# One store of a batched matmul split by partitions, so that one of the 16 DMA engines moves nothing for it

## Chip, cores and metric

One core of one Trainium2 chip. The metric is the device time of one execution in microseconds (us), of the slowest core, which here is the only one. Before: 125.71 us, median of 3 runs (125.65 to 125.92). "Faster" and "slower" mean by over 2%.

## The reference

```python
batch, m, k, n = 16, 512, 512, 512          # a: [16, 512, 512], b: [16, 512, 512], float32
out = np.matmul(a, b.transpose(0, 2, 1))    # float32 [16, 512, 512]
```

33.55 MB are read and 16.78 MB written; one batch of the output is 1 MB, stored as 128 partitions of 8 KB.

## The kernel before

The five engines run hand-written streams that meet at semaphores: SP issues all loads and the stores 8 to 15, POOL issues the stores 0 to 7 through its software queue, DVE casts to bf16, TensorE transposes and multiplies, ACT evicts. The parts that the change and the argument touch:

```python
STORES = "SSSSOSOSOSSOOOOOO"                 # POOL: S = issue the next store, O = wait until one has landed
LATE = {11: (8, 9), 13: (10, 11), 15: (12, 13)}   # SP: stores issued once load 11, 13, 15 has landed

def load(n):                                 # 2 MB: two batches of a (n even) or of b (n odd)
    ...
    nc.sync.dma_start(ld[:, slot], src).then_inc(s_ld[slot], 16)

def landed(n):
    return s_st[n], 16

def store(n):
    engine = nc.gpsimd if n < STORES.count("S") else nc.sync
    engine.wait_ge(s_out, n + 1)
    engine.dma_start(
        out[n].rearrange("(p j) n -> p j n", j=J), ob[:, n % NO]     # 128 partitions x 8 KB
    ).then_inc(s_st[n], 16)
...
for n in range(2 * pairs):                   # SP
    ...                                      # wait for load n, issue load n + 6
    for m in LATE.get(n, ()):
        store(m)
store(batch - 2)
store(batch - 1)
```

Buffer `ob` has seven slots; the slot of store 12 is not written again.

## Time and profile before

| | before |
|---|---|
| time, median | 125.71 us |
| span in the profile | 124.2 us |
| compute done (last eviction ends) | 114.28 us |
| store 15: fifteenth / sixteenth semaphore increment | 120.98 / 122.74 us |
| one 8 KB row on one DMA engine | 0.309 us (one starts 0.306 after the other) |

In the trace each of the kernel's transfers raises its semaphore in 16 increments as its parts land (those of store 15 from 120.60 to 122.74 us); they are read here as one for each of the 16 DMA engines. The times of these increments, and the start and length of every DMA packet, are in the trace; they have no engine number. Times below count from the start of the span. The lines of the profile are in the prediction.

### The profile page before, as it was taken

To read this page: it belongs to the slowest core of one execution; us is meant where nothing else is said; L and a number is where in the kernel's file an instruction comes from. 1 tells how busy PE (TensorE), PEld (TensorE's weight loads), DVE (VectorE), ACT (ScalarE), POOL (GpSimd) and SP (SyncE) were. 2 spreads that over 40 slices of the span, in tenths; PEclk is the share of its full clock that TensorE was granted. 3 is DMA by queue.
4 is the path that set the end of the run, shared out by engine and by line. 5 is a ranking of instruction groups with operands and counts; after the bars stand their busy time and mean duration, and the time that the engine had idled before them with its cause. 6 is when DMAs were issued, how large, how long until landed. Compare 5 with 4: busy or idle time off the path is not lost. (4 is left out here: it accounts for less than half of the span.)

```text
span 124.2 us, 2416 instructions
## 1 busy us (share of the span) xinstructions
PE 92.5 (74%) x768; PEld 58.0 (47%) x768; DVE 70.0 (56%) x112; ACT 68.1 (55%) x130; POOL 6.2 (5%) x14
## 2 busy tenths in 40 slices
PE   0006299998999899899989998995699937995000
PEld 0005296467447644764575477343684426541000
DVE  0055676948992897589488578903968059400000
ACT  4005133679558946966695589435665196556000
POOL 2000000000000070002010220000000000000000
PEclk9999999999999999999999999999779999999965
DMA  4999999999999999999999999999999999999970
GB/s 84 401 425 430 443 438 428 433 428 422 428 428 428 428 438 420 401 430 430 414 425 433 430 438 417 435 435 412 454 414 433 409 430 425 430 430 425 428 327 8
DMA packets 4896, 50.33 MB, mean 405 GB/s; under 512 B 544, under 2 KB 544, under 8 KB 544
## 3 DMA queue, kind: packets, MB, share of 16 engines
q1 hardware_dynamic: 3744, 41.94, 80.2%
q0 software_dynamic: 1152, 8.39, 16.0%
HBM read 33.55 MB, written 16.78 MB: 405 GB/s over the span
## 5 line engine op out<-in xcount | busy, mean ns | idle before, releaser
L266 PE MATMUL ps<-tb,ta 128*128 128x512 bf16 x256 | 57.8, 379 | 0.4
L224 ACT COPY ob<-ps 128x512 f32 x64 | 34.4, 589 | 29.7 <-PE ps L266 26.6
L206 ACT COPY ta<-tp 128x512 bf16<-128x512 bf16 x64 | 32.9, 610 | 15.4 <-PE tp L247 15.4
L266 PEld LDWEIGHTS ps<-tb,ta 128*128 128x128 bf16 x256 | 24.2, 98 | 30.5 <-issue 3.9
L247 PE MATMUL tp<-ident,ha 128*128 128x128 bf16 x256 | 20.2, 236 | 12.6 <-PEq L148 12.6
L247 PE MATMUL tp<-ident,hb 128*128 128x128 bf16 x256 | 19.4, 236 | 8.1 <-PEq L148 7.9
L247 PEld LDWEIGHTS tp<-ident,ha 128*128 128x128 bf16 x256 | 17.5, 107 | 15.8 <-issue 14.1
L187 DVE COPY tb<-tp 128x1024 bf16<-128x1024 bf16 x32 | 21.3, 684 | 5.4 <-DVEq L148 5.3
L247 PEld LDWEIGHTS tp<-ident,hb 128*128 128x128 bf16 x256 | 17.2, 107 | 8.7 <-issue 8.7
L167 DVE CAST hb<-ld 128x1024 bf16 x8 | 5.5, 688 | 12.5 <-DVEq L148 12.3
L182 DVE COPY ha<-wa 128x2048 bf16<-128x2048 bf16 x8 | 5.5, 694 | 10.3 <-DVEq L148 10.1
L167 DVE CAST ha<-ld 128x1024 bf16 x8 | 5.5, 687 | 6.6 <-DVEq L148 6.5
L113 POOL DMA_DIRECT2D out_dram<-ob x8 | 5.5, 693 | 65.0 <-DMA ld<-in_b_dram 41.5
L172 DVE CAST hb<-ld 128x1024 bf16 x8 | 5.5, 685 | 1.1 <-DVEq L148 1.1
L172 DVE CAST ha<-ld 128x1024 bf16 x8 | 5.5, 688 | 1.0 <-DVEq L148 1.0
L186 DVE COPY hb<-wb 128x2048 bf16<-128x2048 bf16 x8 | 5.5, 685 | 0.5 <-DVEq L148 0.5
L170 DVE CAST wa<-ld 128x1024 bf16 x8 | 5.5, 686 | 0.0
L170 DVE CAST wb<-ld 128x1024 bf16 x8 | 5.5, 685 | 0.0
L175 DVE CAST wa<-ld 128x1024 bf16 x8 | 5.5, 684 | 0.0
L175 DVE CAST wb<-ld 128x1024 bf16 x8 | 5.5, 682 | 0.0
L197 ACT ACT_TABLE_LOAD x1 | 1.3, 1283 | 1.1 <-SPq L43 1.1
L80 POOL TENSOR_SCALAR_AFFINE_SELECT ident<-ident 128x128 bf16<-128x128 bf16 x1 | 0.3, 283 | 0.2 <-POOL ident L78 0.2
(6 smaller groups left out, 0.8 us busy)
## 6 DMA issues: line engine op xcount, KB each, us to landing
ld<-in_a_dram SPq DMA_DIRECT2D x7, 2048.0 KB, 29.9
ld<-in_b_dram SPq DMA_DIRECT2D x7, 2048.0 KB, 31.1
out_dram<-ob POOLq DMA_DIRECT2D x8, 1024.0 KB, 28.7
out_dram<-ob SPq DMA_DIRECT2D x8, 1024.0 KB, 20.4
ld<-in_a_dram SPq DMA_DIRECT2D x2, 1024.0 KB, 6.2
ld<-in_b_dram SPq DMA_DIRECT2D x2, 1024.0 KB, 10.2
```

What stands on the lines that cost most here:

```text
L113: engine.dma_start(out[n].rearrange("(p j) n -> p j n", j=J), ob[:, n % NO]).then_inc(s_st[n], 16)
L167: nc.vector.tensor_copy(out=h[:, :J, :], in_=src[:, :J, :HK]).then_inc(s_cd, 1)
L170: nc.vector.tensor_copy(out=w[:, :J, :], in_=src[:, :J, HK:])
L172: nc.vector.tensor_copy(out=h[:, J:, :], in_=src[:, J:, :HK]).then_inc(s_c, 1)
L175: nc.vector.tensor_copy(out=w[:, J:, :], in_=src[:, J:, HK:]).then_inc(s_w, 1)
L182: nc.vector.tensor_copy(out=ha[:], in_=wa[:]).then_inc(s_ca, 1)
L186: nc.vector.tensor_copy(out=hb[:], in_=wb[:]).then_inc(s_cb, 1)
L187: nc.vector.tensor_copy(out=tb[:, ko, :], in_=tp[:, 2 + ko % 2].rearrange("k j p -> k (j p)"),).then_inc(s_eb, 1)
L206: c = nc.scalar.copy(out=ta[:, ko, e * J * P:(e + 1) * J * P].rearrange("k (j p h) -> k j p h", j=J, h=2), in_=tp[:, ko % 2, :, e * HP:(e ...
L224: c = nc.scalar.copy(out=dst[:, j, :].rearrange("m (p j) -> m p j", j=2 * J), in_=ps[:, j, :].rearrange("m (j p) -> m p j", j=2 * J),)
L247: t = nc.tensor.transpose(tp[:, 2 * x + g, j, :], h[:, j, g * P:(g + 1) * P], ident[:])
L266: t = nc.tensor.matmul(ps[:, j, :], ta[:, ko, (e * J + j) * P:(e * J + j + 1) * P], tb[:, ko, :].rearrange("k (j p) -> k j p", j=2 * J)[:, ...
```

## The change: intent and diff

At the end of the kernel before one DMA engine runs 1.76 us behind the fifteen others. The change gives engine 15, taken for that one, nothing to do for one store: 120 partitions were expected to go to fifteen engines and the last eight to eight of these. As the trace has no engine numbers, those in this document are names: 0 to 7 are the eight that also get one of the last eight rows, 8 to 14 the other seven, 15 is the one left out.

```diff
+    FEWER = 12
...
         def landed(n):
-            return s_st[n], 16
+            return s_st[n], 32 if n == FEWER else 16
...
             engine.wait_ge(s_out, n + 1)
+            if n == FEWER:
+                dst, src = out[n].rearrange("(p j) n -> p j n", j=J), ob[:, n % NO]
+                for p, j in ((slice(0, 120), slice(0, J)), (slice(120, P), slice(0, J))):
+                    engine.dma_start(dst[p, j], src[p, j]).then_inc(s_st[n], 16)
+                return
```

## The prediction

> **What bounds the kernel now.** I read the page from the top, then the table of busy time by stretch (the stages, then the last 3 us in slices of 0.2 us), then the increments of each transfer's semaphore. First the page: busy shares, the row of DMA activity and the queues.
>
> ```profile
> span 124.2 us, 2416 instructions
> ...
> PE 92.5 (74%) x768; PEld 58.0 (47%) x768; DVE 70.0 (56%) x112; ACT 68.1 (55%) x130; POOL 6.2 (5%) x14
> ...
> DMA  4999999999999999999999999999999999999970
> GB/s 84 401 425 430 443 438 428 433 428 422 428 428 428 428 438 420 401 430 430 414 425 433 430 438 417 435 435 412 454 414 433 409 430 425 430 430 425 428 327 8
> ...
> q1 hardware_dynamic: 3744, 41.94, 80.2%
> q0 software_dynamic: 1152, 8.39, 16.0%
> ```
>
> No compute engine passes 74%. The 16 DMA engines are full from the second slice to the thirty-eighth, at some 428 GB/s: the kernel moves 50.33 MB and is bound by that. The two queues are the one of SP (all loads, and stores 8 to 15) and the software queue of POOL (stores 0 to 7).
>
> Next, when the compute work ends: the last eviction and the last store's issue, from the timeline.
>
> ```profile
> 113.70 0.58 ACT L224 COPY ob<-ps 128x512 f32 x1
> 114.31 0.33 SPq L113 DMA_DIRECT2D out_dram<-ob  x1
> ```
>
> After 114.64 us only transfers run. The span ends 9.5 us later, so the chain on the page, which stops at this eviction, doesn't show what the end waits for. The table by stretch does (the last two columns are the share of the 16 DMA engines and GB/s; a packet counts in the slice where it starts):
>
> ```profile
> 115.00:118.00 3.00, 0.00 (x0) 0.00 (x0) 0.00 (x0) 0.00 (x0) 0.00 (x0) 1.00 1.02 429
> ...
> 120.00:120.20 0.20, 0.00 (x0) 0.00 (x0) 0.00 (x0) 0.00 (x0) 0.00 (x0) 0.50 0.97 410
> 120.20:120.40 0.20, 0.00 (x0) 0.00 (x0) 0.00 (x0) 0.00 (x0) 0.00 (x0) 0.50 0.60 246
> 120.40:120.60 0.20, 0.00 (x0) 0.00 (x0) 0.00 (x0) 0.00 (x0) 0.00 (x0) 0.50 0.02 0
> 120.60:120.80 0.20, 0.00 (x0) 0.00 (x0) 0.00 (x0) 0.00 (x0) 0.00 (x0) 0.50 0.12 41
> 120.80:121.00 0.20, 0.00 (x0) 0.00 (x0) 0.00 (x0) 0.00 (x0) 0.00 (x0) 0.50 0.00 0
> 121.00:121.20 0.20, 0.00 (x0) 0.00 (x0) 0.00 (x0) 0.00 (x0) 0.00 (x0) 0.50 0.10 41
> 121.20:121.40 0.20, 0.00 (x0) 0.00 (x0) 0.00 (x0) 0.00 (x0) 0.00 (x0) 0.50 0.10 41
> 121.40:121.60 0.20, 0.00 (x0) 0.00 (x0) 0.00 (x0) 0.00 (x0) 0.00 (x0) 0.50 0.00 0
> 121.60:121.80 0.20, 0.00 (x0) 0.00 (x0) 0.00 (x0) 0.00 (x0) 0.00 (x0) 0.50 0.10 41
> 121.80:122.00 0.20, 0.00 (x0) 0.00 (x0) 0.00 (x0) 0.00 (x0) 0.00 (x0) 0.50 0.10 41
> ```
>
> 41 GB/s for 0.2 us is one packet of 8 KB. Up to 120.4 us all engines are at work; after it a single packet starts at a time, five in all, at 120.70, 121.04, 121.35, 121.65 and 121.96 us in the packet records, each of 0.31 to 0.34 us. That is one DMA engine with five rows left when the fifteen others are done: its packets end at 122.27 us, theirs at 120.66.
>
> The semaphore increments say the same, each transfer having 16 of them. Store 15: fifteen from 120.60 to 120.98 us, the sixteenth at 122.74. The instructions end at 124.17, 1.42 us after. Lag of the sixteenth behind the fifteenth, by transfer: 0.12 to 0.15 us in every load that lands before 48.2 us; then 0.40 in the load landing at 70.4, 0.72 at 85.3, 1.02 at 100.2; 1.51 in store 9, 1.71 in store 12, 1.76 in store 15. POOL issues its stores from 43.2 to 72 us and the last lands at 104.8. So the lag is built while the software queue works and is kept afterwards, when every store takes 2.45 us on all engines (eight rows of 0.306 each).
>
> [...] A row here goes at 8192 B / 0.306 us = 26.8 GB/s[...].
>
> **The change part by part.** Removed: the 8 rows of 8 KB that engine 15 moves for store 12, 8 x 0.309 = 2.47 us of its time. Added: one row more on each of engines 0 to 7, 0.31 us; one more issue on SP, 0.33 us by the row of the last store; one more semaphore packet on eight engines, 0.009 us each. Moved: nothing on the four compute engines (the order of their instructions is the same, and store 12's buffer is not written again).
>
> On the path that sets the end: the issue isn't, as stores 12 and 13 are issued some 10 us before their data moves, and store 15 at 114.31 with 3.6 us of rows in front of it (store 14's fifteen increments come by 118.54). The rows are. Engine 15, if it is the laggard, now ends its packets at 122.27 - 2.47 = 119.80. Engines 8 to 14 stay at 120.66 or before, engines 0 to 7 come to 120.66 + 0.31 = 120.97 at most. So the end moves from 122.27 to 120.7-121.0, a gain of 1.3 to 1.6 us. Taken from the landings: 122.74 to 120.98 + 0.31 = 121.29, 1.45 us. The 1.42 us behind the last landing stay. 125.71 - 1.45 = 124.26 us.
>
> **The rivals.**
> (A) *The last eight rows queue [...].* [...] four rows take 4 x 0.309 = 1.24 us in place of 0.31, and 1.55 [...]. Engines 0 to 7 then end at 121.9 to 122.2, and 0 to 0.4 us is left of the gain: 125.3 to 125.7. [...]
> (B) *The 120 partitions collide too.* [...] up to 8 x 0.309 = 2.47 us more for fifteen engines, some 2.1 after the 0.4 us by which the engines are offset. With (A): 120.66 + 2.1 + 1.2 = 124.0 against 122.27, so 1.7 us slower: 127.4. [...] Nothing in the profile speaks for or against.
> (C) *The laggard is another engine.* If it is 7 [...], it gets a row more: 126.0. If it is one of 8 to 14, nothing moves: 125.7. For it: the trace has no number. Against: the change is made to spare the highest engine, and in an already tuned kernel that is hardly by chance.
> (D) *Nothing shows, as the lag is hidden anyway.* Ruled out: nothing but the sixteenth increment holds SP at the end.
>
> **Range and chances.** Main path 124.3 (weight 0.5), A 125.4 (0.2), C 125.8 (0.05), B 127.4 (0.2) and its worst form 129 (0.05). The middle of these lies a little above the main path; I say 124.5, and 124.0 to 127.4 for eight in ten. Faster by over 2% would need under 123.2 us, more than the whole lag of 1.76 gives: 0.02. Slower by over 2% means over 128.2, which only the worst form of B reaches: 0.08. Within 2%: 0.90.
>
> **What would show each step.** Right: in the slices at the end no stretch with one packet at a time; the sixteenth increment of stores 13 to 15 within about 0.5 us of the fifteenth; of the two parts of store 12, the larger landing in about 2.45 us after store 11's; the last landing near 121.3 us. A would show as engines 0 to 7 up to 1.2 us behind engines 8 to 14 in store 13, B as a DMA rate well below 428 GB/s for 2 to 5 us around 111 to 116 us, and packets of over 0.309 us there; C as the same tail of single packets at the end. The prediction is wrong if the compute engines' times move at all, if the rate dips at store 12, or if the lag grows again after it.

## The result, and the profile after

128.70 us (median of 4 runs, 128.52 to 128.98) against 125.70: ratio 1.0237, 95% interval 1.0215 to 1.0260, so slower by over 2%. Ratios here and below are the mean time of one kernel's fast runs over that of the other's of the same rounds, so not quite the ratio of the medians quoted.

The page of the changed kernel, the lines that answer to those of before:

```profile
span 127.2 us, 2417 instructions
...
PE 92.6 (73%) x768; PEld 57.9 (46%) x768; DVE 70.0 (55%) x112; ACT 68.1 (54%) x130; POOL 6.2 (5%) x14
...
DMA  3999999999999999999999999999999999999910
GB/s 88 405 433 446 423 433 443 428 423 417 433 438 433 423 402 438 420 435 397 438 417 443 420 430 428 441 425 428 433 420 425 423 428 425 425 340 402 394 80 10
...
q1 hardware_dynamic: 3751, 41.94, 78.9%
q0 software_dynamic: 1152, 8.39, 15.6%
```

No compute engine's busy time moved by over 0.1 us, and the bytes are the same. SP's queue has 7 packets more (3751 against 3744): 23 semaphore packets (15 and 8) in place of 16, so the transfers do run on 15 and on 8 engines. New are the dip to 340 GB/s in slice 36 and a longer tail. By stretches of 1 us (last two columns: share of the DMA engines that is busy, GB/s):

```profile
110.00:111.00 1.00, 1.00 (x7) 0.42 (x5) 0.00 (x0) 0.84 (x2) 0.00 (x0) 1.00 1.03 434
111.00:112.00 1.00, 1.00 (x6) 0.46 (x5) 0.00 (x0) 0.47 (x1) 0.00 (x0) 1.00 1.02 410
112.00:113.00 1.00, 1.00 (x6) 0.48 (x5) 0.00 (x0) 0.60 (x2) 0.00 (x0) 1.00 1.02 360
113.00:114.00 1.00, 0.51 (x3) 0.01 (x1) 0.00 (x0) 0.80 (x2) 0.00 (x0) 1.00 1.07 303
114.00:115.00 1.00, 0.00 (x0) 0.00 (x0) 0.00 (x0) 0.29 (x1) 0.00 (x0) 1.00 0.92 352
...
121.00:122.00 1.00, 0.00 (x0) 0.00 (x0) 0.00 (x0) 0.00 (x0) 0.00 (x0) 0.50 0.33 139
122.00:123.00 1.00, 0.00 (x0) 0.00 (x0) 0.00 (x0) 0.00 (x0) 0.00 (x0) 0.50 0.14 57
123.00:124.00 1.00, 0.00 (x0) 0.00 (x0) 0.00 (x0) 0.00 (x0) 0.00 (x0) 0.50 0.06 25
124.00:125.00 1.00, 0.00 (x0) 0.00 (x0) 0.00 (x0) 0.00 (x0) 0.00 (x0) 0.50 0.06 25
```

Two things are to be seen. While store 12 moves, the engines stay busy (1.02, 1.07) but move only 303 to 360 GB/s: each packet takes longer. And at the end a single engine is at work (0.06 is one of sixteen; 25 GB/s is one engine's rate, three rows of 8 KB begun in 1 us) until 125.38 us, three microseconds longer than before.

The increments of the stores (fifteenth and sixteenth of the sorted sixteen; us):

```
                       before                 after
            first   15th    16th     first   15th    16th
store 11   110.78  111.22  112.85   110.85  111.12  112.91
store 13   115.72  116.09  117.80   113.53  118.09  120.80
store 14   118.15  118.54  120.26   116.77  120.57  123.26
store 15   120.60  120.98  122.74   119.62  123.00  125.75
```

In store 13 of the changed kernel one engine is done at 113.53, 2.45 us after the punctual group of store 11: it is the engine that skipped store 12, and it was punctual, not late. The late engine got through store 12 like this: 112.91 (store 11), then 117.95 (its share of the 120 partitions), then 118.36 (one of the eight last rows). So it took 5.04 us for eight rows that took 2.50 before, and 0.41 for a ninth that it hadn't had. Chaining its packets (each starts as the one before it ends) gives the rows: 0.35, 0.63, 0.67, 0.61, 0.56, 0.64, 0.63 and 0.91 us, then 0.40. Added: 2.54 + 0.41 = 2.95 us of the 3.0 by which the end moved.

### The profile page after: what moved, and what is told of

Same layout as the page of the kernel before. It is cut to its first block, busy times and chain, and to the rows that moved or that the text cites.

```text
span 127.2 us, 2417 instructions
## 1 busy us (share of the span) xinstructions
PE 92.6 (73%) x768; PEld 57.9 (46%) x768; DVE 70.0 (55%) x112; ACT 68.1 (54%) x130; POOL 6.2 (5%) x14
## 3 DMA queue, kind: packets, MB, share of 16 engines
q1 hardware_dynamic: 3751, 41.94, 78.9%
```

## The experiments

Theory after the result: (1) the late engine is one of engines 0 to 7, so the change gives it a row more; (2) for some choices of partitions two engines get in each other's way ("collide" below) and halve each other. No record names an engine's partitions. So the ranges that the expectations give for (2) are estimates: the measured 0.309 us a row, twice that for the rows assumed to collide. Rivals: the late engine is 15 after all; a transfer on 15 engines, or a second transfer, costs something in itself; the eight last rows carry the loss. Unless a diff says otherwise the edit is to the pair of slices in the changed kernel.

**Which engine is late.** Fifteen small extra stores behind store 12 of the kernel before:

```diff
+            for k in range(1, 16):
+                nc.sync.dma_start(scratch[k, 0:k, 0:N], ob[0:4 * k:4, 12 % NO, 0, :]
+                ).then_inc(s_extra[k - 1], 16)
```

> The kernel before, with fifteen small extra transfers behind store 12 (to a scratch tensor, 2 KB per row, on 1, 2, ... 15 partitions, four partitions apart). If a transfer of k partitions runs on engines 0 to k-1, the landing of each shows whether the engine that is 1.7 us late is among them. My reading of the changed kernel's trace: the late engine also gets one of the last eight rows, so it is one of 0 to 7: the last increment of the probes jumps from about 0.3 us behind the others to about 1.7 us behind at some k of at most 8, and stays there[...]. Rival (the author's intent): the late engine is 15, and all fifteen probes land within 0.4 us. The time grows by under 3 us (engine 0 gets 15 rows of 2 KB, 1.2 us).

Measured: 127.81 us (one run, so its state is unknown; only the order of its increments is read), result correct. Each semaphore gets one increment from SP at the issue (it has to be worth 16 - k, as the kernel waits for 16 and ends), then k more, 3 for k = 3 and 15 for k = 15, so one for each engine; store 12 itself ended with increments at 114.02 and, for the late engine, 115.68:

```
k = 3    113.78  114.20  114.22
k = 4    113.65  113.97  114.38  114.40
k = 5    113.83  114.15  114.56  114.58  115.88
k = 6    114.03  114.16  114.33  114.74  114.77  116.08
k = 15   113.93  113.96 ... 116.36  116.42  117.82
```

Up to k = 4 nothing is late; from k = 5 on one increment is. The late engine is the fifth that these stores take in: engine 4, if they are numbered in that order. It is neither 15, as the change assumes, nor 7. The probes ran on one chip only; in the changed kernel's own trace the late engine also raises the last increment of the eight last rows (118.36), so there too it is one of the first eight.

**Does a second transfer cost?** Same 128 partitions twice, half of each row.

```diff
-((slice(0, 120), slice(0, J)), (slice(120, P), slice(0, J)))
+((slice(0, P), slice(0, J // 2)), (slice(0, P), slice(J // 2, J)))
```

> Control: store 12 as two transfers of all 128 partitions, half of each row (4 KB runs). [...] Two transfers as such cost nothing by every theory but one (that a second transfer or a second set of semaphore increments costs): 125.7 us, within 0.2 us.

Measured: 125.89 us, ratio 1.0008 (0.9985 to 1.0031). Two transfers as such cost nothing that shows.

**The 120 partitions alone** (wrong result, eight rows missing).

```diff
-((slice(0, 120), slice(0, J)), (slice(120, P), slice(0, J)))
+((slice(0, 120), slice(0, J)),)
```

> Wrong result on purpose: the 120 partitions alone, the last eight rows are not stored. [...] most of it stays: in the changed kernel the late engine took 5.05 us in place of 2.45 for its eight rows and 0.40 for the ninth, so about 128.7 - 0.4 = 128.3 us. If the last eight rows carry it (rival A), it is at or below the kernel before, 125.7 us or less.

Measured: 128.01 us, ratio 1.0173 (1.0151 to 1.0194). The late engine took 4.45 us for its eight rows (112.84 to 117.29; 5.04 in the changed kernel). Most of the loss is in the 120 partitions.

**The eight last rows alone**, as an extra store behind store 12 of the kernel before; then with eight partitions four apart.

```diff
+            nc.sync.dma_start(scratch[0, 0:8, :],
+                ob[120:128, 12 % NO]...)     # eight;   eight_spread: ob[0:32:4, 12 % NO]
```

> The kernel before with one extra transfer behind store 12: partitions 120 to 127, 8 KB each, to a scratch tensor. It is the second part of the change alone. Engines 0 to 7, the late one among them, get a row more, 0.31 us; [...] they may take up to 1.2 us, hidden behind the late engine except in the late engine itself. 126.2 to 126.4 us; in the changed kernel this row took the late engine 0.40 us.

> The same with eight partitions four apart (0, 4, ... 28)[...]: one row more on engines 0 to 7[...]. 126.2 us (0.31 more than before), and engines 0 to 7 fall behind the others by just that in store 13, not by up to 1.2 us as in the kernel with partitions 120 to 127.

Measured: 126.37 us (ratio 1.0036, 1.0025 to 1.0046) and 126.51 us (1.0037, 1.0017 to 1.0057). The ninth row costs 0.45 us and more, as the late engine gets it. But the second part of the expectation failed: in store 13 the fifteenth increment came at 116.59 us in the one and 116.68 in the other (116.09 in the kernel before), so eight rows of neighbouring partitions delayed nobody more than eight rows of partitions four apart. Here one row on each of eight engines, behind a whole store of 128 partitions, showed no queue; that isn't so everywhere, as the kernel of 60 + 60 + 4 + 4 below shows (single rows of 1.2 to 2.0 us).

**As many rows on fifteen engines, other partitions.** Four extra stores of 60 partitions behind store 12 of the kernel before: 16 rows more on fifteen engines, 16 x 0.309 = 4.9 us. Only the first partition differs: 0, 36 or 32.

```diff
+            for k in range(4):
+                nc.sync.dma_start(scratch[k, 0:60, :],
+                    ob[0:60, 12 % NO]...     # near60;   far60: ob[36:96];   own60: ob[32:92]
+                ).then_inc(s_extra[k], 16)
```

> The kernel before with four extra transfers of 60 partitions (0 to 59, 8 KB rows, to a scratch tensor) behind store 12: four rows in each on engines 0 to 14. [...] the 16 extra rows of the late engine, 16 x 0.309 = 4.9 us, become about 8.3 us (its partner is 1.6 us ahead [...]): 125.8 + 8.3 = 134.1 us. If a transfer over 15 engines is slow in itself, it is slower than 130.8 too, but then the next kernel is as slow. If neither, 125.8 + 4.9 = 130.7 us.

> The same with partitions 36 to 95: as many rows, bytes, engines and transfers, [...] only the edges of the stretch collide (the late engine [...], up to 1.6 us at half rate): 130.7 to 131.5 us, so about 3 us below the kernel with partitions 0 to 59. If the number of engines is what costs, the two are equal.

> As the kernels with four extra transfers of partitions 0 to 59 (133.7 us) and 36 to 95 (132.6 us, in which one pair of engines ran at half rate all through and the late engine at the end), but with 32 to 91[...]: rows of 0.309 us on every engine and 125.9 + 16 x 0.309 = 130.8 us. [...] some pairs still run at half rate: 132 us or more.

Measured: partitions 0-59 133.65 us (ratio 1.0624), 36-95 132.60 us (1.0534), 32-91 130.91 us (1.0409); none of the 95% intervals is wider than 0.4%. The table by stretch while the extra stores move, first for 0-59:

```profile
115.00:116.00 1.00, 0.00 (x0) 0.00 (x0) 0.00 (x0) 0.00 (x0) 0.00 (x0) 1.00 1.11 270
116.00:117.00 1.00, 0.00 (x0) 0.00 (x0) 0.00 (x0) 0.00 (x0) 0.00 (x0) 1.00 0.93 221
117.00:118.00 1.00, 0.00 (x0) 0.00 (x0) 0.00 (x0) 0.00 (x0) 0.00 (x0) 1.00 1.05 246
118.00:119.00 1.00, 0.00 (x0) 0.00 (x0) 0.00 (x0) 0.00 (x0) 0.00 (x0) 0.82 0.87 205
```

then for 36-95:

```profile
115.00:116.00 1.00, 0.00 (x0) 0.00 (x0) 0.00 (x0) 0.00 (x0) 0.00 (x0) 1.00 0.99 385
116.00:117.00 1.00, 0.00 (x0) 0.00 (x0) 0.00 (x0) 0.00 (x0) 0.00 (x0) 1.00 0.97 385
117.00:118.00 1.00, 0.00 (x0) 0.00 (x0) 0.00 (x0) 0.00 (x0) 0.00 (x0) 1.00 1.05 418
118.00:119.00 1.00, 0.00 (x0) 0.00 (x0) 0.00 (x0) 0.00 (x0) 0.00 (x0) 1.00 1.06 410
```

and for 32-91:

```profile
115.00:116.00 1.00, 0.00 (x0) 0.00 (x0) 0.00 (x0) 0.01 (x1) 0.00 (x0) 1.00 1.03 434
116.00:117.00 1.00, 0.00 (x0) 0.00 (x0) 0.00 (x0) 0.00 (x0) 0.00 (x0) 1.00 1.03 434
117.00:118.00 1.00, 0.00 (x0) 0.00 (x0) 0.00 (x0) 0.00 (x0) 0.00 (x0) 0.81 1.03 434
118.00:119.00 1.00, 0.00 (x0) 0.00 (x0) 0.00 (x0) 0.00 (x0) 0.00 (x0) 0.50 0.97 410
```

The engines are all busy in all three; only the rate differs, by nearly two. In the packet records the rows of partitions 0-59 settle at 0.63 to 0.64 us on fourteen engines, twice 0.309, and stay at 0.309 on two, taken to be one of the fifteen and engine 15, which has no part in these stores. With 32-91 every row takes 0.309, and up to 0.338 on the late engine. With 36-95 two engines run at about 0.61 us a row after their first rows, and the late engine's last four rows take 2.6 us in place of 1.24. I had reckoned with the second and not with the first; why these two run slower isn't shown. The two increments that come last in store 15, at 128.95 and 129.26 us, are over 2.4 us behind the next one (126.47); that pair accounts for the 1.1 us by which 36-95 missed its range. By its rows the one at 128.95 is the late engine, so its loss too (1.4 us) was larger than the 0.8 us that my range allowed. These three kernels refute that fifteen engines cost in themselves, and show that the choice of partitions alone can take a row from 0.309 to 0.63 us. That this is two engines halving each other is the reading of a row twice as long; no record pairs the engines.

**The 120 partitions as two transfers of 60**, meant to keep the engines, the rows on each and the last eight of the changed kernel:

```diff
-((slice(0, 120), slice(0, J)), (slice(120, P), slice(0, J)))
+((slice(0, 60), ...), (slice(60, 120), ...), (slice(120, P), ...))      # landed: 48
```

> Store 12 as partitions 0-59, 60-119 and 120-127: the same engines and as many rows on each as in the changed kernel, the same last eight[...]. The late engine [...] now loses at most half, and with the ninth row 0.4 to 1.5 us: 126.3 to 127.4 us. If the loss comes from fifteen engines with an engine 15 that runs ahead, it stays at 128.7 us.

Measured: 126.45 us, ratio 1.0047 (1.0030 to 1.0063). Other engines still lose (the fifteenth increment of store 15 is at 123.04 us, as in the changed kernel), but the late engine needs 3.16 us for its nine rows, against 5.45, and the end follows it. So most of the 2.5 us on the late engine came from storing the 120 partitions as one transfer and not as two of 60.

**Halves of 64, 96 + 32, and 60 + 60 + 4 + 4.**

```diff
-((slice(0, 120), slice(0, J)), (slice(120, P), slice(0, J)))
+((slice(0, 64), ...), (slice(64, P), ...))       # halves64
+((slice(0, 96), ...), (slice(96, P), ...))       # ninety_six
+(slice(lo, hi), ...) for lo, hi in ((0, 60), (64, 124), (60, 64), (124, P))   # sixties, landed: 64
```

> Store 12 as 64 and 64 partitions: [...] it is slower than before by 1.2 us (four rows of the late engine at half rate) to 2.5 us (all eight): 126.9 to 128.2 us. If it comes from a transfer on 15 engines, or from a row more on engines 0 to 7, it is as the kernel before, 125.7 us.

> Store 12 as 96 and 32 partitions: [...] the late engine (the fifth, as the probes showed) [...] loses some 2.1 to 2.6 us as in the changed kernel (4.60 and 5.05 us for eight rows in place of 2.45): 127.9 to 128.4 us. If the transfer over fifteen engines is what costs: 125.9 us.

> Store 12 as partitions 0-59, 64-123, 60-63 and 124-127: fifteen engines in the two large parts, engines 0 to 3 for the two small ones; engine 15 moves nothing for this store, as in the changed kernel. [...] 125.9 to 126.3 us (others lose over 1 us, hidden behind the late engine). If fifteen engines, or an engine 15 that runs ahead, is what costs: about 128 us.

Measured: 126.01 us (ratio 1.0023, 0.9987 to 1.0059), 126.23 us (1.0023, 1.0011 to 1.0035) and 127.97 us (1.0151, 1.0117 to 1.0184). All three missed the range of theory (2), and all three came near the number that the expectation gave to the rival (125.7, 125.9 and about 128 us). By themselves they would speak for a transfer on fifteen engines as the cost; 32-91 rules that out: there fifteen engines cost nothing extra, with an engine 15 that ran ahead (its store 15 ended at 121.08 us). What the traces show of each:

- Halves of 64: engines do lose time (the fifteenth increment of store 15 comes at 122.56 us in place of 120.98, 1.6 us later), but the loss falls on punctual engines and stays hidden behind the late one, which lost nothing. A loss of up to 1.7 us on any engine but that one is free here (the lag before is 1.76 us).
- 60 + 60 + 4 + 4: the late engine lost at most 0.3 us, as expected (its increments for stores 11 and 12 lie at most 2.78 us apart, 2.50 in the kernel before). But in the two parts of four partitions single rows took 1.2 to 2.0 us, and their engines became the last to end, at 124.94 us. This design didn't isolate what it was to isolate; the two kernels of 60 + 60 + 8 and 32-91 do.
- 96 + 32: the late engine was assumed to collide in all eight rows. It lost at most 0.2 us (increments at 113.00 for store 11 and 115.64 for store 12, 2.64 us), so the assumption doesn't hold here. Why not stays open.

The open end is wider than that one kernel. The late engine was assumed to collide in about four rows with 64 + 64, with 60 + 60 + 8 and with 36-95, and lost 0, some 0.4 and 1.4 us; in the changed kernel, with eight rows assumed, it lost 2.5. Which engines collide, which of two gives way, and after how many rows, no run shows; with 0-59 the first five or six rows after the start still took 0.309 us before the rest took 0.63.

**Does the software queue make the engine late?** All stores from SP; then four of them from POOL.

```diff
-STORES = "SSSSOSOSOSSOOOOOO"
-LATE = {11: (8, 9), 13: (10, 11), 15: (12, 13)}
+STORES = "OOOOOOOOO"                         # half_pool: "SSSSOOOOOOOOO"
+LATE = {2 * i + 3: (2 * i, 2 * i + 1) for i in range(7)}    # half_pool: range(2, 7)
```

> No software queue: all 16 stores go from SP, two of them behind every second load; POOL only counts what has landed. If the lag of one engine is built by the software queue, the sixteenth increment of the last stores comes within 0.3 us of the fifteenth, and the end falls by the lag, 1.5 to 1.7 us: 124.1 us, unless buffers come free too late and the compute falls behind. If the lag is of the engine itself, it stays: 125.8 us.

> Stores 0 to 3 from the software queue of POOL, 4 to 15 from SP. If the lag grows with the number of stores in the software queue, it is about half, 0.8 us, and the time 125.0 us; if it comes with any use of that queue, 1.7 us and 125.8 us.

Measured: 127.55 us (ratio 1.0128, 1.0095 to 1.0160) and 127.21 us (1.0092, 1.0060 to 1.0123). Without a software queue

```profile
q1 hardware_dynamic: 4896, 50.33, 95.7%
```

the last increment of store 15 still comes 1.13 us behind the fifteenth; with four stores in it 1.52; with eight 1.76. So that queue isn't needed for a late engine, though the lag is larger with more stores in it; whether it is the same engine in all three isn't shown. In all three the lag grows while the compute engines run (0.58 to 1.05 from store 7 to 11 without the queue, 1.30 to 1.64 from store 8 to 11 in the kernel before) and changes by at most 0.06 us from store 12 to 15, after TensorE has ended (at 113.5 us before, 114.8 and 115.0 in these two). That the two go together doesn't make one the cause of the other: what slows the engine is open. Both kernels missed every time named in their expectations, because the fifteen others end later, at 123.45 and 121.95 us in place of 120.98; without the queue the DMA rate dipped (295 and 311 GB/s from 50 to 52 us, for one), and the fifteen drifted apart by 2.6 us for a reason that I didn't look into.

No version beat the kernel before.

## Why the prediction was wrong

- *What bounds the kernel, and that one engine ends 1.6 to 1.8 us after the rest:* right. Nothing else moved.
- *"Engine 15, if it is the laggard, now ends its packets at 122.27 - 2.47 = 119.80":* this step failed. The probes put the late engine fifth in the order in which they take engines in, inside the fifteen and inside the eight that get a ninth row. Rival C had the mechanism, at a weight of 0.05; the case against it ("hardly by chance") was an inference from the change's intent, not from the trace. The engine that was spared ended store 15 first, at 119.62 us, where it had no use.
- *"Engines 0 to 7 come to 120.66 + 0.31":* failed too. As in rival B, engines that had been punctual lost up to 2.0 us (store 15's fifteenth increment 123.00, before 120.98). Even had the spared engine been the late one, the end would have been near 123.0, not before 122.74: an estimate from that increment, not a run. This loss alone would eat the gain.
- *Rival B* (eight rows at half rate, up to 2.47 us more) had nearly the right size: 2.54 us on the late engine. Rows at half rate are in the runs of 60 partitions too (0.63 us in place of 0.309 with 0-59); what made B expect them was assumption, which no trace shows. That it fell on this engine in full was not foreseen and isn't explained. What I didn't price was B and C together. I gave B's 2.1 us to punctual engines, where 1.7 us are hidden, and C a single row of 0.31 us. On the late engine both count in full: 2.54 + 0.41 = 2.95 us, 128.7 us. "Only the worst form of B" could reach 128.2, I wrote; their sum did; slower by over 2% had a chance of 0.08. The 129 us of that worst form were the author's estimate, with no trace or run behind them.
- *Rival A*, the last eight rows waiting for one another, four at a time: an assumption, not shown as such. Alone, these rows cost 0.45 us, no more than eight rows of partitions four apart (0.59); in the changed kernel the late engine's took 0.41.
- *"So the lag is built while the software queue works and is kept afterwards":* not borne out. Without the software queue one engine still ended 1.13 us late, and in the kernel before the lag grew from 1.30 to 1.71 us from store 8 to 12, after the last store of that queue had landed.
- *Rival D and the chance of a 2% gain:* rightly ruled out.
- Of the signs named, the dip of the DMA rate at store 12 (303 GB/s) and packets over 0.309 us there pointed to B, and the tail of single packets to C. Both came.

## What to carry to other kernels

When one DMA engine sets the end, find out which one before relieving it: a few tiny transfers on 1, 2, 3, ... partitions, each with its own semaphore, showed it here in one run (one increment late from 5 partitions on). Where a transfer's partition range starts can count as well as its length: here four stores of 60 rows cost 5.0 us or 7.7 us more depending on whether they start at partition 32 or 0. Price two rivals together where they hit the same engine: what is hidden on fifteen engines counts in full on the sixteenth.
